# A plain first pair for three of four feed-forwards, and fewer weights split ahead

## The chip, the cores and the metric

The kernel runs on one core of one Trainium2 chip. The metric is the device time of one execution in microseconds (us), lower is better. A kernel's time is the median of several runs, and one more execution is taken with the profiler.

## The reference

The program is a decoder trunk of two layers over 512 positions of width 1024, in float32:

```python
for l in range(DEPTH):
    x = x + 0.5 * swiglu(rmsnorm(x, ffn1_norm[l]), ffn1_w_gate[l], ffn1_w_up[l], ffn1_w_down[l])
    proj = rmsnorm(x, mix_norm[l]) @ w_in[l]
    ...
    x = x + y @ w_out[l]
    x = x + 0.5 * swiglu(rmsnorm(x, ffn2_norm[l]), ffn2_w_gate[l], ffn2_w_up[l], ffn2_w_down[l])
return rmsnorm(x, final_norm)
```

with `swiglu(x) = (silu(x @ w_gate) * (x @ w_up)) @ w_down` and an inner width of 2816. The part left out is four token mixers (linear attention, a gated recurrence, RWKV-7 and a state-space model), which share one input and one output projection. The change touches the four feed-forwards and the weights of the first mixer stage.

## The kernel before, in words

Activations lie transposed, as eight tiles `x[k]` of 128 channels by 512 positions. A float32 product is made of three half-precision ones: each operand is split into a float16 part (ScalarE, `acopy` or `ACT`, lines 240 to 246) and a bfloat16 rest (VectorE, `TT` or `STT`, lines 213 to 219), and `mm` (line 191) multiplies h by H, h by L and lo by H into one PSUM sum. The gate and up weights of a feed-forward are worked through in eleven pairs of inner blocks. Each pair is a two by two block product: the weight blocks a11, a12 (first block of the pair, lower and upper half of the 1024 channels), a21, a22 (second block), against four quarters of x (half of the channels, half of the positions). It is done with seven products in place of eight, the scheme of Strassen and Winograd: `product` (line 564) is one of the seven, 24 matmuls of 256 columns. The seven need sums of weight blocks (s1 to s4) and sums of quarters of x. The sums s1 and s3 come from memory, since `load_sums` (line 532) adds a second transfer onto the first through GpSimd's queue; s2 and s4 are added on VectorE in `form` (line 547), which also splits a block of 128x1024. `prep_forms` (line 437) makes, for one of four indices j, three plain quarters and the four sums of quarters: four float16 and four rest parts lie in one tile `xf`.

`ffn` (line 606) runs the eleven pairs in a loop (line 652), products and forms in turn, and then the down product: eight output tiles m, each 66 matmuls of 512 columns, after each of which `prep_k` (line 469) makes what the next stage needs of that tile. Feed-forwards are numbered s = 0 to 3. For s = 0 alone the first pair is done plainly before: `direct` (line 593) multiplies the eight whole tiles of x, split by `prep_direct` (line 584), by a11, a12 and then a21, a22 with 512 columns a matmul, and only then come sums. For s = 1 and 3 the last tiles of x come out of the output projection of the mixers (line 1639 and on, eight tiles in the order 0, 4, 1, 5, 2, 6, 3, 7), `prep_k` runs `prep_forms` right behind every second of them, and `pre_ffn` (line 575) loads and forms the first blocks. `pre_ffn` forms a22 of the first pair, and the loop forms it again (line 719); with s = 0 this happens for the second pair.

A second stream of work is mixed in. `pieces` (line 411) splits mixer weights ahead of time: each step loads a piece of 128x512 into a tile `pw`, splits the piece that was loaded two steps ago (float16 part on ScalarE, rest on VectorE, tile `ps`) and writes it to the scratch `w_scr`. Which blocks are split ahead says `AHEAD` (line 36): blocks 3 to 14 of both layers, 48 pieces a layer. With `ahead=3` (lines 1755 and 1758) s = 0 and 2 run three steps a pair, one before the product of s1 and two behind the form of the next a11; the down product runs further steps (line 795). Blocks that are not split ahead are split in the mixer stage by `w_split` (line 377), two halves of 128x1024 each.

The order of the instructions on each engine is not the order of the program text: a scheduler places them at build time, by their place in the text and by when its own model thinks their inputs are there, so that later work may be set ahead of earlier work. Each engine then runs its list in order. SyncE issues nearly all loads, in order as well. Small loads of constants for later stages (`small0`, line 1741, and `norms1`, line 1750) have tiles of their own and nothing that holds them back. For the mixers the text's own order comes from a planner with a model of engine times (`Clock`, line 91).

Of the kernel before, what the change touches and what calls it, by code (L numbers as in the profile page):

```python
# [35 lines left out]
AHEAD = (range(3, 15), range(3, 15))  # L36
# [3 lines left out]
NP = KF // 2  # L40
SY = 2.0 ** -6
# [44 lines left out]
for _name, _w in (("w1", 8), ("w2", 8), ("w3", 8), ("m1", 8), ("m3", 8), ("mu1", 7), ("w0h", 2), ("a0h", 2), ("v0h", 2), ("kah", 2), ("kah1", 2),  # L86
                  ("bah", 2), ("bxh", 2), ("sp4", 2), ("na", 4), ("scw", 24), ("scb", 6)):
    DER[_name] = (_n, _w)
    _n += _w
# [77 lines left out]
def kernel(ctx: ExitStack, tc: tile.TileContext, xT, wffn, wmain, wdown, wsmall, pv_d, pr_d, sm_d, cn_d, outT):  # L167
# [153 lines left out]
    def derive_norm(l):  # L321
        for nm, src, by in (("w1", "ffn1_norm", SX), ("w2", "mix_norm", SX), ("w3", "ffn2_norm", SX), ("m1", "ffn1_norm", -SX),
                            ("m3", "ffn2_norm", -SX)):
            TS(dv(l, nm), pv(l, src, 0, 8), by, MUL)
# [112 lines left out]
    def prep_forms(l, ph, j):  # L437

        wn, mn = (("w1", "m1"), ("w3", "m3"))[ph]
        wa, wb, mb = dv1(l, wn, j), dv1(l, wn, j + 4), dv1(l, mn, j + 4)  # L440
        t = xfp.tile([128, 1792], F32, tag=f"xf{j}", name=f"xf{j}")
        H = t.bitcast(F16)[:, 0:1792].rearrange("p (n t) -> p n t", t=256)
        L = t.bitcast(BF16)[:, 1792:3584].rearrange("p (n t) -> p n t", t=256)
        xa, xb = slot("xa"), slot("xb")
# [13 lines left out]
        xf[j] = (H, L)  # L458

    def prep_sum(k):  # L460
        if k == ORDER[0]:
            acc["t"] = slot("acc")
            ACT(acc["t"], x[k], AF.Square)
        else:
            s = slot("sq")
            ACT(s, x[k], AF.Square)
            TT(acc["t"], acc["t"], s, ADD)

    def prep_k(l, what, k):
# [3 lines left out]
        elif what is not None:  # L473
            if k > 3:
                prep_forms(l, what, k - 4)
# [54 lines left out]
    ra, rb, rc, qs, xd = {}, {}, {}, {}, {}  # L530
# [16 lines left out]
    def form(n, name, steps=1):  # L547
# [6 lines left out]
        if name == "s4":  # L554
            TT(src, src, ra[n][:, 0:1024], ADD)
# [28 lines left out]
    def prep_direct(k):  # L584

        w = dv1(0, "w1", k)
        t = slot("xd")
        h, lo = t.bitcast(F16)[:, 0:512], t.bitcast(BF16)[:, 512:1024]
        ACT(h, x[k], AF.Copy, scale=w)
        STT(lo, x[k], w, h, MUL, SUB)  # L590
        xd[k] = (h, lo)

    def direct(i, a, b):

# [1281 lines left out]
```

## Time and profile before

| what | us |
|---|---|
| median of 3 runs | 1870.83 |
| lowest and highest of them | 1869.82 and 1876.61 |
| the profiled execution | 1876.32 |
| its span, first to last instruction | 1874.2 |
| TensorE busy | 1814.9 (97%) |
| VectorE busy | 1392.5 (74%) |
| ScalarE busy | 987.8 (53%) |
| mean granted TensorE clock | 0.987 |

The stages in the trace, by when TensorE's first matmuls of each begin: s = 0 from 12 us, its down product from 237, the first mixers from 352, s = 1 from 617, s = 2 from 942, the second mixers from 1267, s = 3 from 1532, its down product from 1747. A row of the timeline or the chain gives start and length; a bracket behind it gives the idle time of that engine before it and what ended that idle time. The granted clock is 1.00 at TensorE's upper level (2.4 GHz) and 0.50 at its lower one (1.2 GHz); a stretch's figure is the mean.

### The profile page before, as it was taken

What the parts mean: (1) busy time and instruction counts of PE and PEld (TensorE: products, weight loads), DVE (VectorE), ACT (ScalarE), POOL (GpSimd) and SP (SyncE); (2) the same over time, 40 slices, a digit from 0 to 9 for tenths busy, and PEclk for the clock granted to TensorE, in tenths of its full rate; (3) what the DMA queues carried; (4) which work ended last, traced back from release to release, by engine and by line L of the source; (5) the groups of instructions that cost most, each with busy time, mean ns of one, the idle gap of its engine ahead of it and who ended that gap; (6) DMA issues with size and microseconds to landing.
All of it is one profiled execution on the core that took longest, in us unless ns stands there. A gap on an engine that the chain in (4) does not pass through costs nothing.

```text
span 1874.2 us, 33602 instructions
## 1 busy us (share of the span) xinstructions
PE 1814.9 (97%) x13772; PEld 1268.5 (68%) x13862; DVE 1392.5 (74%) x2274; ACT 987.8 (53%) x1592; POOL 76.9 (4%) x77
## 2 busy tenths in 40 slices
PE   6999999999999999999999999999999989999997
PEld 3888844456865788874488887444577648888544
DVE  7898865467778988886589898344877788888633
ACT  8676754342243676664467776224323547666520
POOL 0000000000010000000000000000000000000000
PEclk9999999999999999999999999999999999999999
DMA  8799757622115676637859993333212255775331
GB/s 290 226 297 276 219 172 244 219 79 67 40 51 173 183 209 214 181 117 256 272 158 278 295 265 126 125 129 116 89 36 67 102 171 163 206 213 134 109 108 45
DMA packets 121705, 314.91 MB, mean 168 GB/s; under 512 B 35152, under 2 KB 61776, under 8 KB 106448
## 3 DMA queue, kind: packets, MB, share of 16 engines
q1 hardware_dynamic: 115360, 267.68, 42.1%
q0 software_dynamic: 6192, 45.09, 12.8%
q8 instruction: 108, 1.77, 0.4%
q14 instruction: 45, 0.37, 0.1%
HBM read 278.11 MB, written 34.62 MB: 167 GB/s over the span
## 4 chain that ended last, share of the span: by engine, by line
PE 75%; DVE 12%; DMA 5%; ACT 4%; issue 3%; SPq 0%; POOL 0%; POOLq 0%; DVEq 0%; ACTq 0%
PE d L192 22%; PE pj L192 9%; PE B L192 9%; PE A L192 9%; PE D L192 4%; PE E L192 4%; PE C L192 4%; PE pt L192 3%; DVE q L214 2%; PE wo L192 2%; DMA pw<-in_wmain_dram 1%; DMA rb<-in_wffn_dram 1%; DMA pv<-in_pv_dram 1%; DVE S L214 1%; DMA ra<-in_wffn_dram 1%
## 5 line engine op out<-in xcount | busy, mean ns | idle before, releaser
L192 PEld LDWEIGHTS <-q 128*128 128x128 f16 (+1 forms) x7336 | 723.3, 99 | 143.0 <-issue 26.1
L192 PE MATMUL d<-h,ws 128*128 128x512 f16 (+3 forms) x2136 | 455.6, 372 | 4.5 <-DVE h L214 1.6
L192 PEld LDWEIGHTS <-ws 128*128 128x128 f16 (+1 forms) x2610 | 254.7, 98 | 297.4 <-issue 7.9
L192 PE MATMUL B<-xf,q 128*128 128x256 f16 (+2 forms) x2072 | 243.4, 277 | 13.1 <-ACT B L241 9.8
L192 PE MATMUL A<-xf,q 128*128 128x256 f16 x2064 | 244.1, 274 | 4.3 <-ACT xf L241 2.3
L214 DVE TENSOR_TENSOR q<-ra,q 128x1024 bf16<-128x1024 f32 (+1 forms) x177 | 211.7, 1205 | 37.7 <-ACT q L245 37.4
L245 ACT CAST ws<-w 128x640 f16<-128x640 f32 (+3 forms) x212 | 118.2, 615 | 198.8 <-PE d L192 76.1
L214 DVE TENSOR_TENSOR ws<-w,ws 128x640 bf16<-128x640 f32 (+3 forms) x212 | 136.8, 688 | 89.0 <-ACT ws L245 87.7
L245 ACT CAST q<-ra 128x1024 f16<-128x1024 f32 (+1 forms) x177 | 181.2, 1029 | 14.0 <-DVE ra L214 7.5
L192 PEld LDWEIGHTS <-w 128*128 128x128 f16 (+1 forms) x864 | 82.7, 99 | 97.9 <-issue 11.3
L192 PE MATMUL pj<-xh,w 128*128 128x512 f16 x448 | 144.0, 384 | 1.9 <-issue 0.4
L192 PE MATMUL D<-xf,q 128*128 128x256 f16 (+2 forms) x1036 | 123.7, 276 | 6.4 <-ACT D L245 5.5
L192 PE MATMUL C<-xf,q 128*128 128x256 f16 (+2 forms) x1036 | 121.2, 273 | 0.0
L192 PE MATMUL E<-xf,q 128*128 128x256 f16 (+1 forms) x1032 | 120.2, 273 | 0.0
L214 DVE TENSOR_TENSOR q<-rb,q 128x1024 bf16<-128x1024 f32 x88 | 107.3, 1221 | 12.8 <-ACT q L245 12.8
L218 DVE SCALAR_TENSOR_TENSOR dx<-d,R 128x512 f32<-128x512 f32 (+1 forms) x33 | 22.3, 675 | 110.4 <-PE d L192 110.4
L241 ACT ACTIVATE th<-S 128x512 f32<-128x512 f32 x88 | 55.5, 630 | 77.2 <-DVE S L214 77.1
L245 ACT CAST q<-rb 128x1024 f16<-128x1024 f32 x88 | 90.8, 1039 | 0.0
L214 DVE TENSOR_TENSOR ps<-pw,ps 128x512 bf16<-128x512 f32 x96 | 63.5, 688 | 17.9 <-ACT ps L245 17.8
L214 DVE TENSOR_TENSOR h<-hf,h 128x512 bf16<-128x512 f32 x88 | 57.6, 689 | 25.5 <-ACT h L245 25.4
L192 PE MATMUL pj<-xl,w 128*128 128x512 bf16 x194 | 73.9, 381 | 0.0
L245 ACT CAST ps<-pw 128x512 f16<-128x512 f32 x96 | 56.6, 614 | 26.6 <-DMA pw<-in_wmain_dram 26.2
(342 smaller groups left out, 2268.3 us busy)
## 6 DMA issues: line engine op xcount, KB each, us to landing
w<-in_wdown_dram SPq DMA_DIRECT2D x64, 704.0 KB, 4.3
ra<-in_wffn_dram SPq DMA_DIRECT2D x87, 512.0 KB, 7.3
rb<-in_wffn_dram SPq DMA_DIRECT2D x43, 1024.0 KB, 6.6
rb<-in_wffn_dram POOLq DMA_DIRECT2D x43, 1024.0 KB, 9.2
pw<-in_wmain_dram SPq DMA_DIRECT2D x96, 256.0 KB, 5.5
w_scr<-ps SPq DMA_DIRECT2D x96, 256.0 KB, 6.0
w<-w_scr SPq DMA_DIRECT2D x24, 1024.0 KB, 4.8
rc<-in_wffn_dram SPq DMA_DIRECT2D x43, 512.0 KB, 4.0
```

The lines of the kernel that those rows point to most:

```text
L192: PE.matmul(out, lhsT, rhs, start=start, stop=stop, skip_group_check=free)
L214: V.tensor_tensor(out=out, in0=in0, in1=in1, op=op)
L218: V.scalar_tensor_tensor(out=out, in0=in0, scalar=scalar, in1=in1, op0=op0, op1=op1)
L241: A.activation(out=out, in_=in_, func=func, scale=scale, bias=bias)
L245: A.copy(out=out, in_=in_)
```

## The change

For s = 0, 1 and 3 (`PLAIN`) the first pair is multiplied plainly, with eight products in place of seven, from quarters of x: `plain` replaces `direct` and works in steps of 256 positions. For these the first loads are the four plain blocks, without the added transfer. The four sums of quarters (`prep_forms`) are made while the plain products run; the plain quarters come first (`prep_first`, and for s = 0 the code at the start). For s = 2 the pair of forms ahead is a11 and s2. The third quarter is no longer negated; s4 is, in `form`. a22 is formed once. For s = 0 a fence of the scheduler alone (`tc.no_sync_barrier`) stands behind the first pair: nothing in the text behind it may be placed ahead of anything before it, on any engine; it is no wait at run time. Layer 0 splits blocks 5 to 14 ahead (40 pieces), no longer 3 and 4; s = 0 and 2 run two steps a pair (`ahead=2`), and in the down product steps run for tiles 1 to 5, two for each first half and, for s = 0 and 2, three for each second half. The order of the first loads of x changes a little.

```diff
-AHEAD = (range(3, 15), range(3, 15))
+AHEAD = (range(5, 15), range(3, 15))
...
+PLAIN = (0, 1, 3)
...
+    def operand(s, w, H, L):
+        ACT(H, s, AF.Copy, scale=w)
+        STT(L, s, w, H, MUL, SUB)
+
+    def prep_first(l, ph, j):
...
+        operand(x[j][:, 0:256], wa, H[:, 0], L[:, 0])
+        if 2 * l + ph in PLAIN:
...
+            operand(x[j][:, 256:512], wa, h, lo)
+            x12[j] = (h, lo)
+        operand(x[j + 4][:, 0:256], wb, H[:, 1], L[:, 1])
+        operand(x[j + 4][:, 256:512], wb, H[:, 2], L[:, 2])
...
-        for n, s, w in ((0, x[j][:, 0:256], wa), (1, x[j + 4][:, 0:256], wb), (2, x[j + 4][:, 256:512], mb)):
-            ACT(H[:, n], s, AF.Copy, scale=w)
-            STT(L[:, n], s, w, H[:, n], MUL, SUB)
...
             if k > 3:
-                prep_forms(l, what, k - 4)
+                prep_first(l, what, k - 4)
+                if 2 * l + what not in PLAIN:
+                    prep_forms(l, what, k - 4)
...
         if name == "s4":
-            TT(src, src, ra[n][:, 0:1024], ADD)
+            STT(src, src, -1.0, ra[n][:, 0:1024], MUL, SUB)
...
-        if step == 0:
+        if step == 0 and s in PLAIN:
+            a, b = (wp.tile([128, 2048], F32, tag="w", name=nm) for nm in ("ra", "rb"))
+            for t, o, c in ((a, 0, 1024), (a, 1024, 2048), (b, 0, 0), (b, 1024, 3072)):
+                dma(out=t[:, o:o + 1024], in_=wffn[s, 0, :, c:c + 1024])
+            ra[0], rb[0], rc[0] = a, b, b[:, 1024:2048]
+        elif step == 0:
             load_blocks(s, 0)
             load_sums(s, 0)
         else:
             form(0, "a11")
-            form(0, "a22")
...
+            form(0, "a12" if s in PLAIN else "s2")
+
+    def plain(i, wa, wb):
+        P = [fbank("P"), bank("P")]
+        for t, p in enumerate(P):
+            for n, nm in enumerate((wa, wb)):
+                h, lo = qs[0, nm]
+                for j in range(4):
+                    X, Y = x12[j] if t and not n else (q[:, (0, 0, 1, 2)[2 * n + t]] for q in xf[j])
+                    for g in range(2):
+                        o, c = p[:, g * 256:(g + 1) * 256], slice(g * 128, (g + 1) * 128)
+                        mm(o, h[:, j, c], X, start=n == 0 and j == 0 and g == 0, stop=False, free=True)
+                        mm(o, h[:, j, c], Y, start=False, stop=False, free=True)
+                        mm(o, lo[:, j, c], X, start=False, stop=n == 1 and j == 3 and g == 1, free=True)
+        return P
...
-            if n == 0 and s == 0:
+            if n == 0 and s in PLAIN:
                 load_sums(s, 1)
                 load_blocks(s, 1)
                 S[0] = wp.tile([128, 2048], F32, tag="w", name="S")
-                pp = [direct(0, "a11", "a12")]
                 form(0, "a21")
+                P = plain(0, "a11", "a12")
                 form(0, "a22")
                 for j in range(4):
-                    prep_forms(0, 0, j)
-                pp.append(direct(1, "a21", "a22"))
+                    prep_forms(l, ph, j)
+                Q = plain(1, "a21", "a22")
                 form(1, "a11")
                 load_sums(s, 2)
-                form(1, "a22")
...
                 sums(ORDER)
...
                 continue
+            if n == 1 and s == 0:
+                tc.no_sync_barrier()
...
-            form(n, "s2")
+            if n > 0 or s in PLAIN:
+                form(n, "s2")
...
-                if 0 < i < 7:
-                    for _ in range(2):
+                if 0 < i < 6:
+                    for _ in range(2 + (keep and q)):
                         next(side, None)
...
-    prep_direct(0)
-    form(0, "a11", 4)
-    for k in range(1, 4):
-        prep_direct(k)
+    xw = [dv1(0, "w1", k) for k in range(KD)]
+    for j in range(4):
...
+        operand(x[j][:, 0:256], xw[j], xf[j][0][:, 0], xf[j][1][:, 0])
+        if j == 0:
+            form(0, "a11", 4)
     form(0, "a12")
-    for k in range(4, KD):
-        prep_direct(k)
+    for j in range(4):
+        for i in range(2):
+            operand(x[j + 4][:, i * 256:(i + 1) * 256], xw[j + 4], xf[j][0][:, 1 + i], xf[j][1][:, 1 + i])
+    for j in range(4):
+        operand(x[j][:, 256:512], xw[j], *x12[j])
...
-    ffn(0, 0, "mix", small0, lambda: derive(0), keep=True, side=split_ahead[0], ahead=3)
+    ffn(0, 0, "mix", small0, lambda: derive(0), keep=True, side=split_ahead[0], ahead=2)
...
-    ffn(1, 0, "mix", lambda: load_small(1), lambda: derive(1), keep=True, side=split_ahead[1], ahead=3)
+    ffn(1, 0, "mix", lambda: load_small(1), lambda: derive(1), keep=True, side=split_ahead[1], ahead=2)
```

## Rows read from the trace of the kernel before

**Rows 1.** The page, busy time of each engine over the span.

```profile
PE 1814.9 (97%) x13772; PEld 1268.5 (68%) x13862; DVE 1392.5 (74%) x2274; ACT 987.8 (53%) x1592; POOL 76.9 (4%) x77
```

**Rows 2.** Stretch, length; busy PE, PEld, DVE, ACT, POOL (instructions); granted clock, DMA share, GB/s.

```profile
35.02:53.40 18.38, 13.62 (x78) 9.98 (x77) 12.12 (x22) 10.75 (x19) 1.94 (x1) 0.72 0.40 113
80.00:140.00 60.00, 59.78 (x548) 53.35 (x547) 55.73 (x67) 42.32 (x63) 3.33 (x4) 1.00 1.01 292
170.00:180.00 10.00, 6.70 (x37) 4.79 (x35) 9.56 (x11) 7.57 (x13) 0.86 (x1) 0.66 0.95 314
245.00:352.00 107.00, 106.04 (x484) 48.23 (x494) 62.76 (x100) 47.48 (x85) 0.00 (x0) 1.00 0.71 230
352.00:617.20 265.20, 259.59 (x2120) 161.33 (x2142) 193.55 (x455) 98.17 (x195) 14.29 (x10) 0.99 0.31 95
617.20:632.60 15.40, 12.14 (x78) 8.69 (x77) 13.97 (x22) 11.56 (x17) 0.86 (x1) 0.78 0.83 226
942.00:1160.00 218.00, 212.81 (x1899) 185.77 (x1899) 197.45 (x250) 158.16 (x234) 11.84 (x14) 1.00 0.78 229
1532.00:1551.00 19.00, 11.61 (x75) 8.01 (x74) 17.70 (x27) 12.49 (x19) 0.86 (x1) 0.82 0.85 225
```

**Rows 3.** The chain that ended last: start, length, what (24 and 50 matmuls).

```profile
57.48 2.62 PE E L192 x24
...
250.47 10.96 PE d L192 x50
```

**Rows 4.** Timeline of the first pair, 0 to 60 us: start, length, engine, what.

```profile
10.65 1.04 ACT L245 CAST q<-ra 128x1024 f16<-128x1024 f32 x1 [0.77 <-DMA ra<-in_wffn_dram]
...
12.38 0.59 PE L192 MATMUL g<-xd,q 128*128 128x512 f16 x1 [12.38 <-ACT xd L241]
...
40.56 0.25 DVE L223 TENSOR_SCALAR der<-pv 128x8 f32<-128x8 f32 x2 [2.34 <-DMA pv<-in_pv_dram]
...
44.18 4.87 PE L192 MATMUL B<-xf,q 128*128 128x256 f16 x22 [2.55 <-DVE q L214]
```

**Rows 5.** Timeline of the first feed-forward, 150 to 185 us.

```profile
169.33 1.04 ACT L245 CAST q<-ra 128x1024 f16<-128x1024 f32 x1 [4.32 <-DMA ra<-in_wffn_dram]
...
173.89 5.28 PE L192 MATMUL D<-xf,q 128*128 128x256 f16 x24 [3.31 <-ACT D L245]
```

**Rows 6.** TensorE's waits in 942 to 1160 us: total, times, longest.

```profile
PE B L192 <- ACT B L241: 2.5, 3, 1.3
PE D L192 <- ACT D L245: 2.0, 2, 1.1
```

**Rows 7.** Timeline of the third feed-forward, 1066 to 1076 us.

```profile
1066.06 1.66 SPq L249 DMA_DIRECT2D pw<-in_wmain_dram  x3
...
1072.49 0.62 ACT L245 CAST ps<-pw 128x512 f16<-128x512 f32 x1 [2.16 <-DMA pw<-in_wmain_dram]
...
1073.64 2.56 PE L192 MATMUL D<-xf,q 128*128 128x256 f16 x22 [1.13 <-ACT D L245]
```

**Rows 8.** Timeline of TensorE where the third feed-forward starts, 920 to 1010 us.

```profile
946.46 2.13 PE L192 MATMUL B<-xf,q 128*128 128x256 f16 x18 [0.67 <-ACT B L241]
```

**Rows 9.** Timeline where the second feed-forward starts, 585 to 650 us.

```profile
624.08 0.58 PE L192 MATMUL B<-xf,q 128*128 128x256 f16 x2 [2.96 <-ACT B L241]
```

**Rows 10.** Timeline where the fourth feed-forward starts, 1486 to 1546 us.

```profile
1533.06 1.23 DVE L214 TENSOR_TENSOR ra<-ra,rb 128x1024 f32<-128x1024 f32 x1 [5.48 <-DMA rb<-in_wffn_dram]
```

**Rows 11.** Instructions by line, shape by shape: busy, mean ns of one, idle before.

```profile
L214 DVE TENSOR_TENSOR q<-ra,q 128x1024 bf16<-128x1024 f32 x173 | 210.3, 1223 | 37.7 <-ACT q L245 37.4
...
L245 ACT CAST ps<-pw 128x512 f16<-128x512 f32 x96 | 56.6, 614 | 26.6 <-DMA pw<-in_wmain_dram 26.2
...
L214 DVE TENSOR_TENSOR acc<-acc,sq 128x512 f32<-128x512 f32 x48 | 33.1, 689 | 4.4 <-ACT sq L241 3.5
...
L218 DVE SCALAR_TENSOR_TENSOR xf<-x,der,xf 128x256 bf16<-128x256 f32 x48 | 21.6, 482 | 5.8 <-ACT xf L241 5.8
...
L214 DVE TENSOR_TENSOR f<-xb,f 128x256 f32<-128x256 f32 x32 | 13.5, 423 | 0.1
```

More of the change, by code (lines that the diff above doesn't have):

```diff
@@ L85 @@
 _n = 0
-for _name, _w in (("w1", 8), ("w2", 8), ("w3", 8), ("m1", 8), ("m3", 8), ("mu1", 7), ("w0h", 2), ("a0h", 2), ("v0h", 2), ("kah", 2), ("kah1", 2),
+for _name, _w in (("w1", 8), ("w2", 8), ("w3", 8), ("mu1", 7), ("w0h", 2), ("a0h", 2), ("v0h", 2), ("kah", 2), ("kah1", 2),
                   ("bah", 2), ("bxh", 2), ("sp4", 2), ("na", 4), ("scw", 24), ("scb", 6)):
@@ L321, in derive_norm @@
     def derive_norm(l):
-        for nm, src, by in (("w1", "ffn1_norm", SX), ("w2", "mix_norm", SX), ("w3", "ffn2_norm", SX), ("m1", "ffn1_norm", -SX),
-                            ("m3", "ffn2_norm", -SX)):
-            TS(dv(l, nm), pv(l, src, 0, 8), by, MUL)
+        for nm, src in (("w1", "ffn1_norm"), ("w2", "mix_norm"), ("w3", "ffn2_norm")):
+            TS(dv(l, nm), pv(l, src, 0, 8), SX, MUL)
     def derive(l):
@@ L581, in pre_ffn @@
             form(0, "a11")
-            form(0, "a22")
[L584 to L593, printed above, removed]
-        p = [fbank("g"), bank("u")]
-        for k in range(KD):
-            h, lo = qs[0, (a, b)[k // 4]]
-            X, Y = xd[k]
-            for g in range(2):
-                c = slice(g * 128, (g + 1) * 128)
-                mm(p[g], h[:, k % 4, c], X, start=k == 0, stop=False)
-                mm(p[g], h[:, k % 4, c], Y, start=False, stop=False)
-                mm(p[g], lo[:, k % 4, c], X, start=False, stop=k == KD - 1)
-        return p
+            form(0, "a12" if s in PLAIN else "s2")
[12 more added lines that the diff above has]
+        return P
     def ffn(l, ph, what, mid=None, mid2=None, keep=False, side=None, ahead=0):
@@ L658, in ffn @@
                 S[0] = wp.tile([128, 2048], F32, tag="w", name="S")
-                pp = [direct(0, "a11", "a12")]
                 form(0, "a21")
+                P = plain(0, "a11", "a12")
                 form(0, "a22")
                 for j in range(4):
-                    prep_forms(0, 0, j)
-                pp.append(direct(1, "a21", "a22"))
+                    prep_forms(l, ph, j)
+                Q = plain(1, "a21", "a22")
                 form(1, "a11")
                 load_sums(s, 2)
-                form(1, "a22")
+                for i, pp in enumerate((P, Q)):
+                    for t in range(2):
+                        acopy(out=quarter(0, i, t), in_=gu(pp[t]))
                 sums(ORDER)
-                for i in range(2):
-                    for g in range(2):
-                        acopy(out=part(0, i, g), in_=pp[i][g])
                 continue
+            if n == 1 and s == 0:
+                tc.no_sync_barrier()
             if n == 0:
@@ L1716 @@
     dma(out=pv_t[0], in_=pv_d[0])
-    a0 = wp.tile([128, 2048], F32, tag="w", name="ra")
-    b0 = wp.tile([128, 2048], F32, tag="w", name="rb")
+    for k in ORDER:
+        x[k] = slot("x")
+    a0, b0 = (wp.tile([128, 2048], F32, tag="w", name=nm) for nm in ("ra", "rb"))
     ra[0], rb[0], rc[0] = a0, b0, b0[:, 1024:2048]
-    for k in range(KD):
-        x[k] = slot("x")
+    dma(out=x[0], in_=xT[:, 0, :])
+    dma(out=a0[:, 0:512], in_=wffn[0, 0, :, 1024:1536])
+    dma(out=x[1], in_=xT[:, 1, :])
+    dma(out=a0[:, 512:1024], in_=wffn[0, 0, :, 1536:2048])
+    for k in range(2, KD):
         dma(out=x[k], in_=xT[:, k, :])
-        if k == 0:
-            dma(out=a0[:, 0:512], in_=wffn[0, 0, :, 1024:1536])
-            dma(out=a0[:, 512:1024], in_=wffn[0, 0, :, 1536:2048])
         if k == 3:
```

27 lines of the change are left out of this document (18 added, 9 removed).

## The prediction

> **What bounds the kernel now.** The page comes first: TensorE is busy 97% of the span [rows 1], so the time is its columns, its gaps, and the stretches in which it runs at the lower level of its clock (1.2 in place of 2.4 GHz). Second, busy time by stretch [rows 2], read for two things: length less PE's busy time is idle, and (1 less the granted clock) times the length is what the lower clock costs, less about half of the idle that falls into it (0.3 to 0.8 us). That gives the losses: behind the first pair of s = 0, 4.76 idle and 5.15 of clock, some 9.4 us; around 174 us 3.30 and 3.40, some 6.2; where s = 1 starts 3.26 and 3.39, some 6.4; where s = 3 starts 7.39 and 3.42, some 10.0; in s = 2 5.19 us of idle with the clock up throughout. Elsewhere little is to be had: the first mixers idle 5.6 us of 265.
>
> Third, what these gaps wait for. TensorE begins at 12.38, on an operand of ScalarE; later it stands for 2.55 us, until 44.18, for a form of VectorE, which itself had stood 2.34 us at 40.56 for the load of a constant of the next layer, `pv`, set into its list too early [rows 4]. The stall at 173.89 hangs on a weight load, used at 169.33 after ScalarE had waited 4.32 us for it [rows 5], with the DMA engines fully taken (share 1.01 from 80 to 140) [rows 2]. In s = 2 the waits are for ScalarE's copies of C and B, 4.5 us [rows 6]; one of them shows the cause: three `pw` loads are issued together at 1066.06, the cast of the third waits 2.16 us for its load, and the copy that TensorE needs is behind that cast in ScalarE's list [rows 7]. Over the kernel ScalarE waits 26.2 us for `pw` [rows 11]. The two seams wait for A to be copied behind a long list of sums: 2.96 us for s = 1 [rows 9], and in s = 3 VectorE stood 5.48 us for the added transfer of `rb` while the last tiles of x queued behind it [rows 10].
>
> **The change, part by part.**
>
> *Columns.* For s = 0 the plain pair has 192 matmuls of 256 columns at 109 ns (2.62 over 24) for 96 of 512 at 219 (10.96 over 50) [rows 3]: 20.9 against 21.0, nothing. For s = 1 and 3 eight products replace seven, 24 matmuls each: +2.62 twice, on the path.
>
> The Trainium skill, TensorE: Matmul & The Clock Gate, Back-to-back issue gap, gives a sustained 131 ns for matmuls of 512 columns, by which 512-wide is much the better form and halving it is wrong. By that figure s = 0 would lose about 8.3 us (20.9 less 96 x 131 ns) and the sum below would be -13.2; the rows show 219 and not 131, so the sum goes by the rows.
>
> *First pair of s = 0.* x is split into sixteen quarters in the order of use, so TensorE can begin near 7 us, but then it is paced: a12 is cast from 10.65 to 11.69 [rows 4], and VectorE then has its rest (1.22) and twelve operands (12 x 0.48 [rows 11]), until 18.7; the last product of the first block follows, so this block ends near 22, and the second, 96 x 109 ns, near 32.5. Before, the pair ended at 35.02, where I cut the first stretch. The next is the fence. VectorE must finish all of the first pair before it adds s2 of the second: from 11.69 that is 1.22, the twelve operands 5.8, forms a21, a22 and the next a11 (3 x 1.22), sixteen sums of quarters (16 x 0.42), four rests (4 x 1.23), seven norm sums (7 x 0.69), the s2 add and its rest (2.45) [rows 11]: 29.4, to 41.1; up to 1.9 us of operands fit in before 11.69, so 39.2. TensorE has meanwhile done the filling matmuls and A, to about 36, and waits again, 3 to 4 us; B starts near 40 and not 44.18. I take -4.2 and no change in the clock's loss. What excludes a repeat of the 2.34 us: the fence puts `pv`'s load behind the first pair's loads in SyncE's list, and its use behind s2's add in VectorE's; SyncE itself does not wait there, so no weight load gets later by it. Bounds: 0 (the new wait is as long as the old) and -11.8 (all of 9.4, plus the pair's end 2.4 earlier).
>
> *Two pieces a pair, in s = 0.* A step splits the piece of two steps ago. With three steps a pair the third splits a piece loaded in the same pair; with two, both were loaded a pair (18 us) earlier, so ScalarE stops waiting for `pw`, and SyncE's writes wait less long in front of `ra`. Each pair moves 0.5 MB less (one load and one write of 256 KB); at 292 GB/s [rows 2] that is 1.7 us less to queue behind, and it adds up from pair to pair. I take the whole 6.2, for the wait of 4.32 us had a queue as its cause; bounds 0 and -6.2.
>
> *The same in s = 2.* Of the 4.5 us on copies [rows 6], 0.67 is the first pair's own [rows 8] (its A ends and the copy takes that long, with no product of an earlier pair between); -3.8, bounds 0 and -4.8.
>
> *Where the pieces go.* Layer 0 needs 42 steps: 20 in the gate-up pairs, 22 in the down product, where 25 fit; layer 1 has 20 in s = 1, 20 in s = 2, 10 in its down product. Cover: a down stretch of 107 us with VectorE busy 62.8 and ScalarE 47.5 [rows 2], before a TensorE at work for 106. Nothing; without the cover 1.3 us a piece.
>
> *Two blocks split in the first mixers.* Four forms more, 4 x 1.22 = 4.9 us of VectorE and 4.2 of ScalarE, under a stage in which VectorE is busy 193.6 of 265 [rows 2]; the planner's order changes with it. Between 0 (all hidden) and +4.9 (all on the path) no row is nearer: +2.5.
>
> *Starts of s = 1 and 3.* The plain pair needs no sum of x and no added transfer; behind the last x only two quarters (2 x 0.48) stand before products that cover them. The sums move to the 21 us of the plain products, and GpSimd's queue has one added transfer less ahead of the second pair's. What is late next is s2 of the second pair: with nothing done beforehand VectorE has one x (0.69), four operands (1.9), three forms (3.7), sums and rests (11.6), norm sums (4.8), s2 (2.45): 25.1 us, against a cover of 8 x 2.62, four filling matmuls (4 x 0.219) and A's 2.62 = 24.5. That is even; but a21, a22 and three of the four sets can be made during the output projection, in which VectorE no longer has the sums (4 x 0.42 + 1.23 a set). So the wait left is the copy of A, 0.67. s = 1: -6.4 + 2.62 + 0.67 = -3.1; s = 3: -10.0 + 3.3 = -6.7. Bounds: without the copy's wait -3.8 and -7.4; with a stall like the one behind today's first pair (9.4) +5.6 and +2.0.
>
> *Together:* the second form of a22 goes (four times 1.22 of VectorE, off the path), s4 by one instruction of the same length, two small constants less: nothing, hidden under TensorE.
>
> Sum: -4.2 - 6.2 - 3.8 + 2.5 - 3.1 - 6.7 = -21.5. The profiled execution took 1876.3 and would take 1854.8. It stands 5.5 us above the median, so against the median of 1870.83 I predict 1849.
>
> **Rivals.** *Seams give little.* If the sums, moved behind the plain pair, leave a wait as long as the old one at each seam, and the fence does the same in s = 0, the pieces still pay: -6.2 - 3.8 + 2.5, s = 1 at -0.1 (-6.4 + 2.6 + 3.7), s = 3 at -3.7: -11.3, 1860. For it: the even sum of 25.1 and 24.5.
>
> *The pieces do not pay either.* DMA stays full and the stall only moves (0 and 0), the two blocks' forms lie on the path (+4.9), the first pair gives its -4.2 and the seams half (-1.5 and -3.3): -4.1, 1867. For it: the share of 1.01; against it: the wait is one of order and not of volume [rows 7].
>
> *VectorE becomes the bound.* It is busy 55.7 of 60 us in s = 0's pairs [rows 2]. If that sets the pace, taking waits away gains nothing there (0, 0, 0), the mixers pay 4.9, and at both seams the 25 us come in late, by enough to drop the clock, 9.4 each (+5.6 and +2.0): +12.5, 1883. It decides where VectorE's list from the last x to s2 takes over 24.5 us. Against it: TensorE loses 0.2 us in those 60.
>
> *512-wide is cheaper.* If a matmul of 512 columns cost much less than two of 256, the 192 small ones of s = 0 would make its first pair longer. The 219 ns are against it [rows 3]. The page of the Trainium skill named above is the one that has it so; by its figure the sum is -13.2 and the time 1858.
>
> **How the numbers follow.** Forecast 0.56, seams give little 0.20, pieces do not pay 0.14, VectorE 0.09, 512-wide 0.01. About 0.5% (9.4 us) is what a measurement can tell. The forecast is faster, as are two thirds of the second case: 0.70; slower is the VectorE case, 0.09; the rest, 0.21, is within. The range: downwards all bounds together reach -34; I stop at 1838; upwards it takes in the third case at 1867. That leaves out the fourth case and some of the tails, under 2 in 10.
>
> **What would show it.** TensorE's first matmul near 7 us, the plain pair over near 32.5, B near 40; no wait of ScalarE for `pw` in the pairs and no stall near 170; s = 1 and 3 with eight products in a row, then under 1 us of wait before B, and the clock at 1.00 there; the first mixers near 265 us. Wrong: VectorE ending s2 over 25 us after the last x, idle over 2 us ahead of B with a granted clock of 0.5, or mixers longer by 5.

## The result, and the profile after

The changed kernel takes 1852.76 us (median of four, 1850.40 to 1854.53) where the kernel before, on the same chip, takes 1872.12 (1869.82 to 1876.61): a ratio of 0.9893, 95% interval 0.9869 to 0.9917. Run again later, with six runs against eleven, it gave 1850.58 against 1869.28: 0.9898, 0.9878 to 0.9918. So it is faster by 1.0 to 1.1%, some 19 us. The profiled execution took 1854.53 us. The page begins so:

```profile
span 1852.8 us, 33924 instructions
...
PE 1815.9 (98%) x14006; PEld 1278.3 (69%) x14006; DVE 1378.0 (74%) x2252; ACT 978.6 (53%) x1578; POOL 73.7 (4%) x75
```

The page counts 234 matmuls of TensorE more than before [rows 1], but 90 of them are records that the trace before lacks (its page has 13862 weight loads and 13772 matmuls; here both are 14006). So 144 are new: 96 in s = 0 and 24 each in s = 1 and 3. TensorE has 1.0 us more of work in a span 21.4 us shorter: what was gained is idle time and half clock (stretches at a granted clock of 0.50). The busy time by stretch (stretch; length; PE, PEld, DVE, ACT, POOL busy with counts; granted clock; DMA share; GB/s) shows where:

```profile
6.81:42.33 35.52, 29.64 (x228) 23.35 (x229) 31.17 (x65) 29.33 (x51) 1.90 (x2) 0.99 1.01 343
42.33:53.44 11.11, 11.11 (x76) 8.82 (x76) 8.98 (x20) 5.51 (x10) 1.94 (x1) 0.74 0.42 148
80.00:140.00 60.00, 60.00 (x552) 53.78 (x550) 53.71 (x60) 42.31 (x59) 2.59 (x3) 1.00 0.90 255
170.00:180.00 10.00, 10.00 (x94) 8.97 (x93) 8.62 (x11) 7.02 (x11) 0.69 (x1) 1.00 0.87 217
341.68:610.01 268.33, 261.98 (x2142) 162.93 (x2140) 200.10 (x461) 104.41 (x205) 14.64 (x10) 0.99 0.31 99
610.01:816.48 206.47, 206.47 (x1890) 184.81 (x1889) 172.52 (x200) 139.78 (x196) 8.06 (x9) 1.00 0.59 173
930.99:1136.40 205.41, 204.39 (x1866) 182.44 (x1865) 184.90 (x228) 149.29 (x215) 8.88 (x10) 1.00 0.76 225
1136.40:1255.49 119.09, 115.97 (x531) 52.09 (x528) 64.08 (x102) 46.70 (x84) 2.99 (x4) 0.99 0.51 170
1518.92:1725.39 206.47, 206.47 (x1889) 184.81 (x1888) 174.04 (x202) 140.98 (x199) 8.93 (x10) 1.00 0.59 170
```

Set against [rows 2]: the stretch 170 to 180 is full, at full clock (6.70 of 10 busy at 0.66 before); the DMA share of 80 to 140 fell from 1.01 to 0.90; s = 1 and s = 3 are without a gap from their first matmul to their last, at clock 1.00. Beside the first mixers, which idle 6.4 us (5.6 before), two stretches still lose time: the start of s = 0, and the down product of s = 2 (1136.40 to 1255.49), which idles 3.1 us.

The first column of the next table counts from the first matmul of a stage to the first of the next, as the two timelines have them.

| stage | before | after | difference |
|---|---|---|---|
| to the first matmul | 12.38 | 6.81 | -5.57 |
| gate and up, s = 0 | 224.59 | 219.55 | -5.04 |
| its down product | 115.37 | 115.32 | -0.05 |
| first mixers | 264.87 | 268.33 | +3.46 |
| gate and up, s = 1 | 210.42 | 206.47 | -3.95 |
| its down product | 114.51 | 114.51 | 0 |
| gate and up, s = 2 | 210.10 | 205.41 | -4.69 |
| its down product | 114.60 | 119.09 | +4.49 |
| second mixers | 265.58 | 263.43 | -2.15 |
| gate and up, s = 3 | 214.21 | 206.47 | -7.74 |
| the rest | 127.6 | 127.4 | -0.2 |
| span | 1874.2 | 1852.8 | -21.4 |

The start, in the timeline (start, busy us, engine, line, operation; in brackets the idle time ahead and what ended it):

```profile
6.81 1.81 PE L194 MATMUL P<-xf,q 128*128 128x256 f16 x7 [6.81 <-ACT q L247]
...
30.65 2.78 PE L194 MATMUL P<-xf,q 128*128 128x256 f16 x24
...
32.97 4.67 DVE L216 TENSOR_TENSOR sq<-sq 128x512 f32<-128x512 f32 x6
33.27 0.59 PE L194 MATMUL B<-xf,q 128*128 128x512 f16 x2
...
37.55 1.22 DVE L216 TENSOR_TENSOR ra<-ra,rb 128x1024 f32<-128x1024 f32 x1
...
38.86 1.99 ACT L247 CAST q<-ra 128x1024 f16<-128x1024 f32 x2 [3.47 <-DVE ra L216]
...
41.71 0.57 ACT L243 ACTIVATE B<-A 128x512 f32<-128x512 f32 x1
...
42.33 5.28 PE L194 MATMUL B<-xf,q 128*128 128x256 f16 x24 [3.53 <-ACT B L243]
...
53.44 2.78 PE L194 MATMUL E<-xf,q 128*128 128x256 f16 x24
```

Read it from the bottom. B (42.33) waits 3.53 us for ScalarE's copy of A. A's own matmuls ended near 36.9; the copy stands in ScalarE's list behind casts for the second pair; the first of these casts waits 3.47 us for VectorE's addition for s2 (37.55), and that addition stands in VectorE's list behind six norm sums. A wait in the order of a list has taken the place of the wait for `pv` [rows 4].

The waits of TensorE over the whole span (what waited, for what: us, times, longest) put the down product of s = 2 next:

```profile
PE P L194 <- ACT q L247: 6.8, 1, 6.8
PE B L194 <- ACT B L243: 4.2, 2, 3.5
PE d L194 <- ACT h L247: 3.3, 2, 2.7
```

### The profile page after: what moved, and what is told of

It reads as the page before. It is cut to its first block, busy times and chain, and to the rows that moved or that the text cites. A ratio compares the mean times of both kernels' runs of the same rounds, so it can differ in the third digit from the quotient of the medians.

```text
span 1852.8 us, 33924 instructions
## 1 busy us (share of the span) xinstructions
PE 1815.9 (98%) x14006; PEld 1278.3 (69%) x14006; DVE 1378.0 (74%) x2252; ACT 978.6 (53%) x1578; POOL 73.7 (4%) x75
## 4 chain that ended last, share of the span: by engine, by line
PE 88%; DVE 6%; ACT 2%; issue 2%; DMA 1%; POOL 0%; SPq 0%; POOLq 0%; DVEq 0%; ACTq 0%
PE d L194 23%; PE B L194 11%; PE A L194 11%; PE pj L194 10%; PE C L194 5%; PE D L194 5%; PE E L194 5%; PE wo L194 3%; PE pt L194 3%; PE P L194 2%; PE z L194 1%; PE go L194 1%; DVE h L216 1%; PE yo L194 1%; DMA w<-in_wdown_dram 1%
## 5 line engine op out<-in xcount | busy, mean ns | idle before, releaser
L194 PEld LDWEIGHTS <-q 128*128 128x128 f16 (+1 forms) x7480 | 734.0, 98 | 104.9 <-ACT q L247 8.0
L194 PEld LDWEIGHTS <-ws 128*128 128x128 f16 (+1 forms) x2706 | 264.4, 98 | 313.6 <-issue 14.9
L194 PE MATMUL B<-xf,q 128*128 128x256 f16 (+2 forms) x1976 | 227.4, 275 | 4.5 <-ACT B L243 4.2
L194 PE MATMUL A<-xf,q 128*128 128x256 f16 (+1 forms) x1968 | 228.9, 273 | 0.0
L194 PEld LDWEIGHTS <-w 128*128 128x128 f16 (+1 forms) x768 | 73.6, 99 | 86.3 <-issue 9.8
L194 PE MATMUL pj<-xh,w 128*128 128x512 f16 x384 | 122.9, 381 | 0.0
L194 PE MATMUL D<-xf,q 128*128 128x256 f16 (+2 forms) x988 | 115.6, 273 | 0.0
L194 PE MATMUL C<-xf,q 128*128 128x256 f16 (+2 forms) x988 | 115.6, 273 | 0.0
L194 PE MATMUL E<-xf,q 128*128 128x256 f16 (+1 forms) x984 | 114.6, 273 | 0.0
L194 PE MATMUL pj<-xh,ws 128*128 128x512 f16 x224 | 69.5, 379 | 0.0
```

The source lines that it names most:

```text
L194: PE.matmul(out, lhsT, rhs, start=start, stop=stop, skip_group_check=free)
```

## The experiments

Each kernel is the changed one with the edit shown. The first four share a chip, so do the next four and the last three, with medians of before at 1870.08, 1868.96 and 1869.28 us there. Where medians lie closer than about 3 us, as those of before do from chip to chip, the verdict is read from stages of the profile.

**The fence left out.**

```
-            if n == 1 and s == 0:
-                tc.no_sync_barrier()
```

> The fence behind the first pair of the first feed-forward is left out; nothing else is changed. Theory (the fence keeps other work out of the first pair's tail): without it the loads and the arithmetic of constants that are needed only later are placed among the first pair's work again, as they were in the kernel before, where a wait of 2.34 us for them stood ahead of the second pair; TensorE's matmul B of the second pair, at 42.33 us with the fence, comes 2 to 4 us later, and the time rises by 2 to 4 us. Rival (the fence itself costs): what the second pair needs no longer stands behind the norm sums (32.97 to 37.55 us on VectorE), B comes at 38 to 39 us, and the time falls by 4 to 7 us. If neither matters, B stays within 1 us of 42.33 and the time within 2 us of the changed kernel's 1852.8.

Measured: 1850.81 us (1850.32 to 1853.51), ratio 0.9906 (0.9884 to 0.9929). Its timeline, VectorE's rows first:

```profile
33.21 1.23 DVE L216 TENSOR_TENSOR ra<-ra,rb 128x1024 f32<-128x1024 f32 x1 [2.76 <-DMA rb<-in_wffn_dram]
...
50.15 0.23 DVE L225 TENSOR_SCALAR der<-pv 128x8 f32<-128x8 f32 x2
```

```profile
38.95 0.39 PE L194 MATMUL E<-xf,q 128*128 128x256 f16 x2 [3.16 <-ACT q L247]
39.43 4.57 PE L194 MATMUL B<-xf,q 128*128 128x256 f16 x24
...
50.32 2.57 PE L194 MATMUL E<-xf,q 128*128 128x256 f16 x22
```

The theory fell. The constants from `pv` stand at 50.15 without the fence (51.70 with it), far from the 40.56 of the kernel before [rows 4], so it is not the fence that keeps them away. The addition for s2 comes at 33.21 instead of 37.55, and E, counted from the first matmul, 2.9 us earlier (50.32 less 6.63, against 53.44 less 6.81). That is the rival in kind, though TensorE still waits 3.16 us for a cast, B comes at 39.43 and not at 38 to 39, and the fall of 4 to 7 us did not come: the median is 2.0 us below the changed kernel's first and 0.2 above its second, and the ratio is no lower.

**The norm sums behind s2 of the second pair.** `sums(ORDER)` leaves the first pair for s = 0:

```
             if n > 0 or s in PLAIN:
                 form(n, "s2")
+            if n == 1 and s == 0:
+                sums(ORDER)
```

> The norm sums of the first feed-forward (eight squares on ScalarE, seven additions on VectorE) move from the end of the first pair to the second pair, behind the forming of its first sum. Theory (in the order of the lists the sum s2 of the second pair waits behind the norm sums, 32.97 to 37.55 us, and B behind s2): the addition for s2 comes at about 33 us, B at 38 to 39 instead of 42.33, and the time falls by 3 to 7 us (up to 3.4 of it from a shorter half clock). Rival (B waits for ScalarE's copy of A or for a load and not for VectorE's order): B stays within 1 us of 42.33. Second rival: the norm's root then comes late and the second pair's scaling waits: B is early, but the gain of 3 to 7 us is lost by the third pair, where TensorE then waits for a product's sums.

Measured: 1850.40 us (1850.24 to 1853.26), ratio 0.9903 (0.9884 to 0.9922). The addition for s2 comes at 33.14, B at 39.16, E at 49.93: 3.2 us earlier by the same count, with the fence in place. Its timeline:

```profile
35.40 3.22 ACT L243 ACTIVATE sq<-x 128x512 f32<-128x512 f32 x6
...
38.53 0.57 ACT L243 ACTIVATE B<-A 128x512 f32<-128x512 f32 x1
...
39.16 4.45 PE L194 MATMUL B<-xf,q 128*128 128x256 f16 x24 [3.08 <-ACT B L243]
```

The mechanism of the theory holds: with the norm sums out of its way, s2 is early whether the fence stands or not, so the order of VectorE's list delayed it in the changed kernel, and not the fence as such, nor a load (its own, `rb`, lets it start by 33.2 in both kernels). But B still waits 3.08 us, now because ScalarE's copy of A stands behind six squares for the norm in ScalarE's list; the first rival had that part. Of what E gains, 1.7 us are half clock (3.4 us of it, not 6.8) and some 1.3 are idle time. The gate and up part is 1.7 to 2.4 us shorter than in the changed kernel's two profiles (217.14; 218.79 and 219.55), and the median is 2.4 and 0.2 us below its two, short of the 3 to 7.

**Only the first feed-forward plain.**

```
-PLAIN = (0, 1, 3)
+PLAIN = (0,)
```

> Only the first feed-forward keeps its plain first pair; the second and the fourth begin with the seven sums again, as in the kernel before. Theory (the plain pair takes the seam between two stages away): the second feed-forward's gate and up part goes from 206.5 back to about 210.4 us, the fourth's from 206.5 to about 214.2, the clock falls to half for some 7 us behind each of their starts, and the time rises by 10 to 12 us. Rival (the gain in these two stages comes from something else in the change, such as the fewer reads of DRAM or the shorter list of constants): the two stages stay within 1 us of 206.5 and the time rises by under 3 us.

Measured: 1858.21 us (1857.22 to 1859.15), ratio 0.9941 (0.9923 to 0.9959); 5.5 us above the changed kernel's first median, 7.6 above its second, and 8 to 9 by the ratios. Half of the theory holds. At s = 3 TensorE's timeline shows the loss at the seam between the two stages again, just ahead of the stage:

```profile
1517.06 5.07 PE L194 MATMUL wo<-y,ws 128*128 128x512 f16 x12 [4.86 <-DVE x L220]
1521.96 0.60 PE L194 MATMUL B<-xf,q 128*128 128x512 f16 x2
...
1526.30 2.13 PE L194 MATMUL B<-xf,q 128*128 128x256 f16 x18 [0.69 <-ACT B L243]
```

The clock is at half from 1515.0 to 1521.8, and second mixers and s = 3 together take 476.52 us, against 469.9 in eight of the eleven profiles with the plain pair there (up to 471.9 in the other three): 6.6 us is what it is worth there. At s = 1 the sum shows no such thing: first mixers and s = 1 together take 475.25, against 474.80 with it (475.29 before). There is a seam (TensorE waits 2.2 us, and 3.4 us run at half clock), but it is smaller than before, where 3.26 us were idle and 6.8 at half clock, and without the plain pair 24 matmuls, 2.62 us, are saved.

**No step in the last pair.**

```
-            if n > 0 and ahead:
+            if n > 0 and ahead and not last:
                 next(side, None)
```

> The one step of the side work (a piece loaded, split and written back) that stands in the last pair of the first and the third gate and up part is left out there; it runs in the down product behind it instead, so nothing is computed differently. Theory (the write of a piece stands on SyncE ahead of the load of a down block, and holds ScalarE's cast of it and so the late halves of h): the third down product goes from 119.1 back to about 114.6 us, the wait of 2.69 us for h and the half clock of 3.4 us at 1147 us are gone, the rest stays, and the time falls by 3 to 5 us. Rival (that stall is chance, of a load that took 6.5 us where others took 4.8): the third down product may be anywhere between 114.6 and 119.1 us in either kernel, and the times of several runs agree with the changed kernel's within 1.5 us. Second rival: the step itself is what TensorE lacks time for, and the down product takes it over at its own cost: no gain, 0 to 2 us more.

Measured: 1851.35 us (1848.02 to 1853.59), ratio 0.9903 (0.9882 to 0.9924). The median lies between the changed kernel's two (1.4 us below, 0.8 above). The down product of s = 2 takes 114.60 us, but in the other kernels here that split two pieces a pair and keep the step it takes 115.3 to 115.6. How the 119.09 came about, the changed kernel's timeline shows:

```profile
1126.12 0.52 SPq L251 DMA_DIRECT2D w_scr<-ps  x1
...
1126.68 17.36 SPq L251 DMA_DIRECT2D w<-in_wdown_dram  x4
...
1133.24 1.35 ACT L247 CAST ws<-w 128x640 f16<-128x640 f32 x2 [3.11 <-DMA w<-in_wdown_dram]
...
1134.97 2.69 ACT L247 CAST h<-hf 128x512 f16<-128x512 f32 x5
...
1146.37 0.38 PE L194 MATMUL d<-h,ws 128*128 128x512 f16 x1 [2.69 <-ACT h L247]
```

SyncE issues the write of a piece (it waits for VectorE's half of the piece) and only then the load of a down block; ScalarE waits 3.11 us for that load, the splits of h are behind its cast, and TensorE waits 2.69 us for h and then runs 3.4 us at half clock. The same kernel, run again (below), shows the same order with a load that lands 1.4 us sooner after its issue:

```profile
1126.23 25.62 SPq L251 DMA_DIRECT2D w<-in_wdown_dram  x5
...
1131.37 1.35 ACT L247 CAST ws<-w 128x640 f16<-128x640 f32 x2 [1.70 <-DMA w<-in_wdown_dram]
...
1144.11 0.38 PE L194 MATMUL d<-h,ws 128*128 128x512 f16 x1 [0.88 <-ACT h L247]
```

So theory and first rival are each half right: the step in the last pair puts the load where a late landing reaches TensorE; it cost 0.7 to 1.0 us in six profiles and 4.5 in one.

**Three pieces a pair, as before.**

```
-AHEAD = (range(5, 15), range(3, 15))
+AHEAD = (range(3, 15), range(3, 15))
-                if 0 < i < 6:
-                    for _ in range(2 + (keep and q)):
+                if 0 < i < 7:
+                    for _ in range(2):
```

and `ahead=3` for 2 in both calls.

> The pieces as the kernel before had them (three steps a pair, all twelve blocks of both layers, two steps a half in the down products); the plain pairs, the fence and all else as in the changed kernel. Theory (with three steps a piece is asked for and split inside one pair, so that ScalarE waits for its load and TensorE for ScalarE): the wait near 170 us comes back, with half clock behind it; the first gate and up part goes from 217 to 219.6 us back to 223 to 226, the third from 205.4 to 209 to 210.1; the mixers of the first layer, which no longer split two blocks, fall by 1 to 3.5 us, the third down product stands at 114.6; the sum is 6 to 10 us above the changed kernel's 1850 to 1853. Rival (the plain pair has put the loads elsewhere and the room is enough): no wait over 1 us for a piece, both parts within 1 us of the changed kernel's, and the time is lower by 1 to 4 us.

Measured: 1853.12 us (1851.21 to 1856.94), ratio 0.9919 (0.9894 to 0.9943). s = 2 takes 211.07 us against 205.41 in every kernel with two pieces, and its timeline has the pattern of [rows 7]:

```profile
1072.29 1.60 SPq L251 DMA_DIRECT2D pw<-in_wmain_dram  x3
...
1078.19 0.62 ACT L247 CAST ps<-pw 128x512 f16<-128x512 f32 x1 [1.64 <-DMA pw<-in_wmain_dram]
...
1079.35 2.78 PE L194 MATMUL D<-xf,q 128*128 128x256 f16 x24 [0.85 <-ACT D L247]
```

In s = 0, from the second pair's E to the down product, it takes 176.35 us against 172.92: +3.4. The wait near 170 us that the theory expected did not come: TensorE's longest wait in these pairs is 1.7 us, at 110.71, and the clock stays up. And the first mixers fall from 268.33 to 264.34. The net is 0.4 to 2.5 us by the medians and 4 to 5 by the ratios, less than the theory's 6 to 10.

**Three pieces, split three steps behind their loads.**

```
-        for n in range(len(todo) + 2):
+        for n in range(len(todo) + 3):
-            if n > 1:
+            if n > 2:
-                dma(out=todo[n - 2][1],
+                dma(out=todo[n - 3][1],
```

on top of the edit above.

> As three pieces a pair on all blocks, but each piece is split three steps behind its load instead of two, so that no split is in the same pair as its load; the work is the same. Theory (order: the wait is for a load asked for too late): no wait over 1 us for a piece, the first gate and up part within 1.5 us of the changed kernel's 217 to 219.6 and the third within 1 of 205.4, so the time is 0 to 4 us below the changed kernel's. Rival (volume: VectorE, or the transfers, have no time for a third piece): the two parts stay 3 to 6 us longer, as with three pieces and a lag of two, and the time 5 to 10 us above.

Measured: 1852.92 us (1852.39 to 1854.07), ratio 0.9916 (0.9894 to 0.9938). The two stages part here. s = 2 takes 206.53 us: of the 5.66 that the third piece costs there, 4.5 were the wait of a split for its own load, and 1.1 are left. In s = 0 the same stretch takes 177.95, not less than with a lag of two; its timeline:

```profile
148.69 1.89 SPq L251 DMA_DIRECT2D w_scr<-ps  x3
150.64 2.27 SPq L251 DMA_DIRECT2D ra<-in_wffn_dram  x2
...
162.70 1.05 ACT L247 CAST q<-ra 128x1024 f16<-128x1024 f32 x1 [5.27 <-DMA ra<-in_wffn_dram]
...
167.27 4.45 PE L194 MATMUL D<-xf,q 128*128 128x256 f16 x24 [3.20 <-ACT D L247]
```

ScalarE waits for a weight load, as in [rows 5], with the DMA share at 0.97 from 80 to 140 us (0.90 with two pieces). That looks like volume, but another order is left which the longer lag does not touch. SyncE issues this load behind three writes of pieces, 7.7 us after TensorE's E of the pair (142.94), and it lands 12.0 us after its issue. In the changed kernel SyncE's list has it ahead of the writes, 2.0 us after E (145.14), and it lands 6.6 us after its issue:

```profile
147.12 0.61 SPq L251 DMA_DIRECT2D ra<-in_wffn_dram  x1
...
150.90 1.18 SPq L251 DMA_DIRECT2D w_scr<-ps  x2
```

All ten profiles with two pieces have the load ahead of the writes there and no stall; the three with three pieces have it behind two or all three of them, and two of these stall (before and here). In the third, the kernel with a lag of two, it landed 6.0 us after its issue. Whether its place in the list or the fuller DMA decides was not tried.

**All blocks ahead, two pieces a pair.**

```
-AHEAD = (range(5, 15), range(3, 15))
+AHEAD = (range(3, 15), range(3, 15))
-                if 0 < i < 6:
-                    for _ in range(2 + (keep and q)):
+                if 0 < i < 7:
+                    for _ in range(3 if keep else 2):
```

> Two steps a pair as in the changed kernel, but all twelve blocks of the first layer are split ahead; the eight more steps stand in the first down product (six a row block instead of five, and one row block more). Theory (the two blocks split in the mixers cost ScalarE and VectorE time on the path there): the first mixers fall from 268 to 270 us to 265 to 267, nothing else moves, the time falls by 1 to 3.5 us. Rival (the mixers hide the two splits, and their spread of 267 to 270.5 comes from stretches at half clock): the mixers stay within that spread and the time within 1.5 us of 1850 to 1853. Second rival (the first down product has no room for six steps): it goes over its 115.3 us by 2 to 6, and the time rises by 1 to 4 us.

Measured: 1853.10 us (1850.65 to 1853.74), ratio 0.9913 (0.9891 to 0.9936). The first down product takes 117.18 us (+1.9) and TensorE waits 1.8 us for the operand of the first projection behind it, with half clock from 348.1 to 354.9; the mixers take 270.03. The second rival comes nearest, at the low end of its 2 to 6 us: that down product has no room for six steps. What two blocks cost in the mixers is better read from TensorE's waits there, first in the changed kernel, then in the one with three pieces, which splits all blocks ahead:

```profile
PE yt L199 <- DVE xD L216: 2.8, 2, 1.8
```

```profile
PE yt L199 <- DVE xD L216: 0.2, 1, 0.2
```

This wait is the same 2.8 us in all nine profiles that split the two blocks in the mixers, and 0.2 in all four that split them ahead: 2.6 for the two blocks. All rows of these two views sum to 6.5 and 2.7 us, but such sums differ from kernel to kernel, 5.6 to 7.6 with the two blocks and, but for the late first operand above, 2.7 to 4.6 without.

**The second feed-forward not plain.**

```
-PLAIN = (0, 1, 3)
+PLAIN = (0, 3)
```

> The second feed-forward begins with the seven sums as in the kernel before; the first and the fourth keep the plain pair. Theory (in the second the plain pair takes a wait from the start of its gate and up part and puts as much into the end of the mixers ahead, which must prepare the quarters): mixers and gate and up part of the first layer together take 474 to 477 us, as in the kernel before (475.3) and the changed one (474.8); the time stays within 2 us of the changed kernel's 1850 to 1853. Rival (the plain pair pays here as predicted, 3.1 us or more): the sum of the two is 478 or more and the time rises by 3 to 5 us.

Measured: 1848.20 us (1846.73 to 1849.61), ratio 0.9892 (0.9865 to 0.9919). First mixers and s = 1 together take 471.75 us: not more than with the plain pair, less. It is also below the theory's 474 to 477: here the mixers ran without any half clock; elsewhere they had 3.4 to 10.2 us of it. In s = 1 itself TensorE waited 2.2 us, with the clock up, nearly all of it here:

```profile
611.44 2.12 PE L194 MATMUL B<-xf,q 128*128 128x256 f16 x18 [2.02 <-ACT B L243]
```

That wait is about what 24 matmuls of the plain pair, 2.62 us, cost. The predicted gain of the plain pair in s = 1 isn't seen.

**The changed kernel once more, and two kernels that join the edits.** The first has no edit:

> The changed kernel once more, as the measure for the two beside it. If the 4.5 us that its third down product took above 114.6 were the chance of one late load, that product takes 115.3 to 115.5 us here, as in the other kernels with the same order, and the median is 1850 to 1852; if it belongs to the kernel, it takes about 119 again and the median is 1852.8.

Measured: 1850.58 us (1848.87 to 1853.77); the down product of s = 2 takes 115.59. The second drops the step in the last pair and moves the norm's parts in s = 0 further back:

```
             product(B[n % 2], n, "s2", 5, start=False)
+            if n == 1 and s == 0:
+                sums(ORDER)
...
             product(A[n], n, "a12", 1, start=False)
+            if n == 1 and s == 0:
+                r = norm_sum(1.0 / SX)
...
             product(m5, n, "s1", 4)
+            if n == 1 and s == 0:
+                R = norm_spread(r)
```

> Two edits on the changed kernel: no step of the side work in the last pair, and the norm sums of the first feed-forward further back than in the earlier try, behind the second pair's product B, with the norm's own small steps behind the products of A and E. Theory (the second pair waits in the order of the lists behind the sums): B at 37 to 39 us, E at 48.5 to 50 against 53.4, at most 3.4 us of half clock there, the third down product at 114.6; the time is 3 to 5 us below the changed kernel's in the same call. Rival (the wait only moves: with the sums further back the norm's root is late, and the second pair's scaling and the pair behind it wait): E is early, but the products up to 70 us take it back, and the time is no lower than with the sums just behind s2, 0 to 2.5 us below the changed kernel's.

Measured: 1848.32 us (1847.38 to 1850.36), ratio 0.9885 (0.9866 to 0.9904). Its timeline:

```profile
33.73 1.23 DVE L216 TENSOR_TENSOR ra<-ra,rb 128x1024 f32<-128x1024 f32 x1 [1.50 <-DMA rb<-in_wffn_dram]
...
38.01 0.58 ACT L243 ACTIVATE B<-A 128x512 f32<-128x512 f32 x1
...
38.64 2.78 PE L194 MATMUL B<-xf,q 128*128 128x256 f16 x24 [1.14 <-ACT B L243]
...
48.33 2.78 PE L194 MATMUL E<-xf,q 128*128 128x256 f16 x24
```

With the squares out of ScalarE's list too, B waits 1.14 us instead of 3.53, the clock does not fall there at all, and E comes 5.0 us earlier than in the changed kernel (41.64 after the first matmul, not 46.63). The whole of s = 0's gate and up part is 3.2 us shorter than in the repeat (215.59, 218.79), the two down products 0.7 and 1.0. The theory holds for these stages, and the wait at the start of s = 0 is one of order on both engines. But of the 4.9 us the median shows 2.3: the profile has half clock in the second mixers here (1451.0 to 1457.8, some 2 us) and none in the repeat. The third kernel adds `PLAIN = (0, 3)`:

> As the kernel with the two edits, and besides the second feed-forward begins with the seven sums again, as in the kernel before. Theory (the plain pair there costs 2.62 us of TensorE and the preparing of quarters at the end of the mixers, and saves no more than that): the time is 2 to 4 us below that with the two edits. Rival (the low time of the kernel with the plain pair in the first and the fourth alone was the mixers' running without any half clock, by chance): the time is within 1.5 us of that with the two edits, and the mixers with the second gate and up part take 474 to 477 us again.

Measured: 1846.62 us, the lowest median of all, ratio 0.9891 (0.9864 to 0.9918); but two of its six runs took 1854.8 and 1855.0, so the mean (1848.9) is no lower than the kernel's above. First mixers and s = 1 take 477.26 us, by the rival. Its profile is 3.0 us shorter than that of the kernel above, but in s = 0 (1.6) and the second mixers (2.1), which this edit does not touch. The best that the experiments support is the kernel with the two edits; whether the plain pair in s = 1 should go stays unclear.

## Why the prediction was right, and where its terms were off

The sum, -21.5, met the spans (-21.4). The medians differ by 19.4, and the time is 3.8 us above the 1849 predicted. Of these, 2.1 are the smaller difference: the sum was made against a profiled execution that stood 5.5 us above its median, and taken from the median whole. Another 1.3 are the median before, 1872.12 with the fourth run and not 1870.83. That the sum itself was met so closely is partly luck, as the terms show:

- *Columns, and 512 against 256.* Right. The second half of the plain pair runs without a gap, 24 matmuls in 2.62 us (30.65 to 33.27), 109 ns each, as predicted from [rows 3]. The Trainium skill, TensorE: Matmul & The Clock Gate, Back-to-back issue gap, gives a sustained 131 ns for 512 columns; the rows here do not agree (219 ns, [rows 3]), and the rival that leaned on it fell.
- *First pair of s = 0, -4.2.* The start near 7 (6.81) and the pair's end near 32.5 (33.27) were right; B near 40 was not (42.33, -1.85). Up to E it is -4.0, since half clock fell there from 10.2 to 6.8 us, which I had left out; that the total came out is luck. The step that failed: I counted the norm sums into VectorE's work ahead of s2 (29.6 us by its items, not 29.4) but not that ScalarE's copy of A would stand behind the casts in its own list, 2.9 us after the first of them (38.86 to 41.71). Nor is it the fence that keeps `pv` away: its constants are late without it, and why was not tried.
- *Two pieces a pair, -6.2 in s = 0.* From E to the down product -6.6. Three pieces in the changed kernel cost only 3.4 there, though. The traces show the difference: before, it was one stall, 3.31 us of waiting [rows 5] and 6.8 us of half clock behind it; with three pieces in the changed kernel that stall did not come, with a load that landed 6.0 us after its issue where before's, at the same place, took 12.9, and shorter waits of 2.8 us in sum did, at full clock. That a third piece costs time in s = 0 is shown; that the cause is volume, as I had it, is not: SyncE's order is left as a rival. There are 19 steps in these pairs, not 20: the last pair has one.
- *The same in s = 2, -3.8.* -4.7; order, as I had it from [rows 7], shown by the lag of three (4.5 of 5.66).
- *Where the pieces go, 0.* Right for s = 0 (-0.05), wrong for s = 2 (+4.49 in this profile, +0.7 to 1.0 in the others). I named VectorE and ScalarE as the cover, and not SyncE, whose list holds a piece's write ahead of a down block's load.
- *Two blocks in the mixers, +2.5.* +2.6 by the one wait that comes and goes with them; +3.46 by the stage, in which the place of the half clock differs too.
- *Seams.* s = 1 -3.95 and s = 3 -7.74, for -3.1 and -6.7: even the copy's 0.67 is hidden. For s = 3 the experiment confirms it (6.6). For s = 1 it doesn't: measured with the mixers ahead, the plain pair's gain there was not seen. The term that was mis-sized is the 6.4 of the old seam. More than half of it, 3.4 us, was clock, and without the plain pair three profiles show 2.2 to 2.6 us of waiting there and 3.4, 0 and 0 us of half clock, where before had 6.8.
- *Second mixers, no term.* -2.15: before, the clock was at half from 1469.9 to 1476.8 (0.83 granted from 1460 to 1480), after it was not. I take this for chance: three of the twelve later profiles have half clock at the same place, some 204 us into the stage (one of them 1451.0 to 1457.8, above), and the others have none there. It cancels half of the dear down product of s = 2, and the terms that came out larger than forecast cancel the rest; that is the luck in the sum.

Of the rivals, "seams give little" was right in kind at s = 0, where the fence left a wait of 3.53 for one of 2.55, and by the experiments at s = 1; it was wrong at s = 3. "The pieces do not pay either" did not come: a third piece put back costs 3.4 us in s = 0 and 5.7 in s = 2. "VectorE becomes the bound" did not come: 53.7 busy of 60, TensorE 60.0.

## What to carry to other kernels

When work is moved behind a new point in the program, write out each engine's list from that point, ScalarE's copies too: the sum of VectorE's work was about right here, and the copy behind the casts decided. A split that is done ahead can cost by order (a load asked for and used in one pair, or a write set ahead of a weight load) and by volume. A longer lag takes away the first of these alone, so what remains under it is not yet volume. A term is judged over the stage and its neighbour together: a plain first pair that made s = 1 gapless had no gain left once the mixers ahead were counted. And half clock that a seam shows in one execution should not be counted whole as its price.

## What was not expected of the hardware

The same program drops its clock in different places. The stretch 540 to 552 in the first mixers, first in the changed kernel's profile, then in its repeat:

```profile
540.00:552.00 12.00, 12.00 (x94) 8.21 (x91) 8.15 (x14) 1.23 (x2) 1.63 (x1) 0.72 0.01 1
```

```profile
540.00:552.00 12.00, 12.00 (x131) 8.03 (x130) 9.24 (x17) 3.07 (x6) 1.63 (x1) 1.00 0.05 8
```

The granted clock is 0.72 in one and 1.00 in the other, and TensorE gets 94 and 131 matmuls done; the repeat has its half clock from 415.5 to 418.9 instead, where the first has none. Whole-stage lengths of the mixers therefore differ by some 5 us between kernels that are alike there (264.71 and 269.86 us in the two with `PLAIN = (0, 3)`), and terms of 2 to 4 us are read from waits. And one load of a down block, at the same place in the list, landed 6.5 us after its issue in one execution and 5.1 in the other.
